# Pooling groups taken in the opposite order, and sums of late modulation vectors folded at wider spacing, in a single-core transformer layer

## The chip, the core and the metric

The kernel runs on one core of a Trainium2 chip. The core has five engines that work side by side: TensorE (PE) multiplies matrices, VectorE (DVE) and ScalarE (ACT) work on whole tiles element by element, GpSimd (POOL) does the same more slowly and issues some of the DMAs, and SyncE (SP) issues the others. Each engine takes its instructions in the order of its own queue. The metric is the time of one execution on the device, in microseconds (us).

## The reference, cut to what matters

The layer updates 256 latent tokens of width 2048, with 256 context tokens beside them. All arithmetic is float32.

```python
mod = silu(c) @ w_mod + b_mod                    # six vectors of 2048: sa, ca, ga, sm, cm, gm
h   = rmsnorm(x) * (1 + ca) + sa                 # the context tokens get their own sa, ca
p   = h @ w_in                                   # q, k, v, pooling input u, gate logits
heads = rmsnorm(diff_attention(q, k, v))         # 8 heads, two softmaxes each
# pooling: u is split in four groups of 256 channels, windows w = 2, 4, 8, 16
for g, w in enumerate((2, 4, 8, 16)):
    lo, hi = clip(t - w // 2, 0, L), clip(t + w - w // 2, 0, L)
    d[g] = window_sum(u[g], lo, hi) / (hi - lo) - u[g]
    y[g] = (d[g] @ pool_w[g]) * pool_scale[g]
mix = (sigmoid(gate_a) * (heads @ w_a_up) + sigmoid(gate_b) * (y @ w_b_up)) @ w_o
x = x + ga * mix
x = x + gm * relu((rmsnorm(x) * (1 + cm) + sm) @ w_ff1) ** 2 @ w_ff2
```

Near either end of the sequence a window is cut off, so that the sum is divided by fewer tokens than w.

## The kernel before, in words

**Products and weight chunks.** Nearly all the time goes into products with weights that are read once. A weight comes as chunks of 128 x 1024 float32 numbers (512 KB). The list `stream`, written by `plan` (L128 to L173), fixes the order of all chunks. For each chunk SP loads a tile `raw` (L117), ACT rounds it to a high part `whi` (L245), and DVE subtracts to get the low part `wlo` (L246). A product is then three products on PE: high by high, high by low and low by high (`mm3`, L276 to L278, and `xstat`, L454 to L460). `wchunk` hands out the next chunk; two chunks ahead of it are loaded and split by then.

**The stages.** Modulation (sa, ca) with the first q and k columns; v, q, k; then, from about 310 us in the trace, `pooling` (16 chunks of w_p), `gates` (four rounds of w_gb_in, w_b, w_ga_in, w_a), the output projection w_o, and the MLP in eight blocks (`ff1`, `ff2`). Attention runs beside the bulk products from v to the first gates: after a fixed amount of bulk work `run` (L870) takes one more step of `attention`. Every second head its clamped squares (`osq`, L727, on POOL) go through a product with a matrix of means (`osum`, L731) for the head norm.

**Pooling.** For a group, four chunks of w_p give u in one PSUM bank (`pin`). ACT copies it into two padded tiles `za` (L786), and POOL adds shifted copies (L791): one add per tile for a window of 2, two for 4, three for 8, four for 16. Some chunks later `pool_diff` does the edge operation on DVE: it multiplies the first w/2 columns (L802) and the last w/2 - 1 columns (L804) by w over the true count, and takes sum / w - u (L806). A window of 2 has no last columns, so its group has no L804. One chunk on, the difference is split into high and low (`split`, L272 and L273), and `pool_out` multiplies it by pool_w. `pool_out` of a group is called two groups later, the last two in the first gates.

**Late modulation.** The vectors ga, cm, sm and gm are needed late, so their weights are slipped between the other chunks at set rates (`late_gen`). DVE multiplies each chunk by its part of silu(c) and adds it up in a tile of 128 partitions (L627, L629), in two halves of 1024 columns per vector. The sum over the 128 partitions is made by seven accumulating DMAs on POOL's queue (`late_fold`, L634), each of which adds the lower half of the partitions that are left to the upper: 64, 32, 16, 8, 4, 2, 1. Then the sum is added to the bias row in DRAM (L637) and broadcast back (L640). Each of these needs the one before to have landed, and POOL waits for that before it issues it. The row's bias is loaded by L619.

**What sets the order.** `later(n, fn)` runs fn when n more chunks have been handed out (`tick`), so it sets the place of fn's instructions in the traced program. From the traced program a planner makes each engine's queue, by when it expects an instruction's operands to be ready; a later traced instruction may go ahead of an earlier one. `pin` holds an instruction behind the one traced just before it on its engine. L802, the additions L627 and L629, the transposes of attention and `osum` are pinned; L804, L806, the splits, POOL's adds and the folds are not.

Of the kernel before, what the change touches and what calls it, by code (L numbers as in the profile page):

```python
# [12 lines left out]
F32R = mybir.dt.float32r  # L13
# [4 lines left out]
P = 128  # L18
# [9 lines left out]
WINDOWS = (2, 4, 8, 16)  # L28
# [20 lines left out]
def layer(ctx: ExitStack, tc, a, out):  # L49
# [22 lines left out]
    def bank(name):  # L72
        return psum.tile([P, 512], F32, tag="ps", name=name)

    def work(name, shape=None, dt=F32):
        return pool.tile(shape or [P, 512], dt, tag="w2", name=name, bufs=9)

    def s16(name, shape, dt=F32):
        return pool.tile(shape, dt, tag="s16", name=name, bufs=7)

    def s8(name, shape, dt=F32):
        return pool.tile(shape, dt, tag="s8", name=name, bufs=2)
# [4 lines left out]
    def pairtile(name):  # L87
        return s16(name, [P, 2, 8, T], F32R)
# [4 lines left out]
    credit_rate = [0.0]  # L93
# [3 lines left out]
    def later(n, fn):  # L97

        waiting.append([n, fn])
# [28 lines left out]
    def plan(name, *idx, rate=0.0):  # L128
        stream.append(((name,) + idx, rate))
# [15 lines left out]
    for n, g, rate in (("w_v", 0, 0.75), ("w_q", 1, 1.0), ("w_k", 1, 1.0), ("w_v", 1, 0.75)):  # L145
        for ch in range(8):
            plan(n, g, ch, rate=0.0 if (n, g) == ("w_v", 1) and ch < 3 else rate)
    for g in range(4):
        for i in range(4):
            plan("w_p", 2 * g + i // 2, i % 2, rate=0.6)  # L150
            if g > 1 and i == 1:
                plan("pool_w", g - 2)
    for g in range(4):
        for n, nk in (("w_gb_in", 8), ("w_b", 4), ("w_ga_in", 8), ("w_a", 4)):
            for ch in range(nk):
                plan(n, g, ch, rate=0.66)
                if g == 0 and n == "w_gb_in" and ch in (1, 7):
                    plan("pool_w", 2 if ch == 1 else 3)
    for g in range(4):
        for ch in range(8):  # L160
            plan("w_o", g, ch, rate=0.6 if g < 2 else 0.0)
# [138 lines left out]
    def pr(name):  # L300
        lo, hi = PRM[name]
        return prm[:, lo:hi]
# [251 lines left out]
    for f in range(KT):  # L554
        if f % 2 == 0:
            ps = bank("mod")
# [40 lines left out]
    def late_gen():  # L597
        for name in ("ga", "cm", "sm", "gm"):
            if name == "ga":
                dst = ga_bc  # L600
            elif name == "gm":
                mods["gm"] = None
                yield
                mods["gm"] = s8("gm_bc", [P, D])
                dst = mods["gm"]
            else:
                if "sb" not in mods:
                    mods["sb"] = s16("sb", [P, 2, D])
                dst = mods["sb"][:, 0 if name == "cm" else 1, :]
            for half in range(2):  # L610
                yield
                o = dst[:, half * 1024:half * 1024 + 1024]
                norm_w = pr("nmw")[:, 8 * half:8 * half + 8] if name == "cm" else None
                for k in range(KT):
                    raw = raw_chunk(a["w_" + name][half, k])
                    later(2 if credit_rate[0] < 1 else 1, partial(late_part, o, raw, k))
                    if k == 8:
                        row = rows.tile([1, 1024], F32, tag="row", name="row")
                        nc.gpsimd.dma_start(row, a["b_" + name][half])  # L619
                    if k == KT - 1:  # L620
                        later(2 if credit_rate[0] < 1 else 1, partial(late_fold, o, row, norm_w, P // 2))
                    yield

    def late_part(o, raw, k):
# [3 lines left out]
        else:  # L628
            pin(vec.scalar_tensor_tensor(o, raw, sil[:, 0, k:k + 1], o, ALU.mult, ALU.add))  # L629

    def late_fold(o, row, norm_w, n):

        if n > 0:
            nc.gpsimd.dma_start(o[0:n, :], o[n:2 * n, :], accum_op=ALU.add)  # L634
            later(2, partial(late_fold, o, row, norm_w, n // 2))
            return
        nc.gpsimd.dma_start(row, o[0:1, :], accum_op=ALU.add)  # L637
        if norm_w is not None:
            later(1, partial(late_norm, row, norm_w))
        later(2 if norm_w is None else 3, lambda: nc.gpsimd.dma_start(o, row.broadcast_to([P, 1024])))  # L640
# [117 lines left out]


    ybh = [None]  # L760
    diff = []

    def pooling():
        yb = pairtile("yb")
        ybh[0] = yb
        diff.clear()
        for g, w in enumerate(WINDOWS):
            ps = bank("pin")
            for i in range(2):
                for kc in range(2):  # L770
                    hi, lo = wchunk("w_p", 2 * g + i, kc)
                    for kk in range(8):
                        k = 8 * kc + kk
                        sl = slice(kk * P, kk * P + P)
                        mm3(ps[:, i * T:i * T + T], hi[:, sl], lo[:, sl], act_slice(hL, k, 0), act_slice(hL, k, 1),
                            k == 0, k == KT - 1)
                    if g > 1 and i == 0 and kc == 1:
                        pool_out(g - 2)
                    yield 2
            s0 = 8 - w // 2  # L780
            sums = []
            for i in range(2):
                src = work("za", [P, T + 16])
                gp.memset(src[:, 0:8], 0.0)
                gp.memset(src[:, T + 8:T + 16], 0.0)
                act.copy(src[:, 8:T + 8], ps[:, i * T:i * T + T])  # L786
                step, n = 1, T + 16
                while step < w:
                    n -= step

                    gp.tensor_add(src[:, 0:n], src[:, 0:n], src[:, step:step + n])  # L791
                    step *= 2
                sums.append(src[:, s0:s0 + T])
            later(3 if g < 3 else 6, partial(pool_diff, g, w, ps, sums))

    def pool_diff(g, w, ps, sums):

        d = work("d")
        n0, n1 = w // 2, w // 2 - 1
        e0 = PRM["edge"][0] + sum(x - 1 for x in WINDOWS[:g]) * 2  # L800
        for i, s in enumerate(sums):
            pin(vec.tensor_mul(s[:, 0:n0], s[:, 0:n0], prm[:, e0:e0 + n0]))  # L802
            if n1:
                vec.tensor_mul(s[:, T - n1:T], s[:, T - n1:T], prm[:, e0 + n0:e0 + n0 + n1])  # L804
            sl = slice(i * T, i * T + T)
            vec.scalar_tensor_tensor(d[:, sl], s, 1.0 / w, ps[:, sl], ALU.mult, ALU.subtract)  # L806
        diff.append((work("dh", dt=F32R), work("dl", dt=F32R)))
        later(1, partial(split, *diff[-1], d))

    def pool_out(g):  # L810
        dh, dl = diff[g]
        wh, wl = wchunk("pool_w", g)
        pd = bank("pd")
        for i in range(2):
            for k in range(2):
                sl = slice(k * T + i * P, k * T + i * P + P)
                mm3(pd[:, i * T:i * T + T], wh[:, sl], wl[:, sl], dh[:, k * T:k * T + T],
                    dl[:, k * T:k * T + T], k == 0, k == 1)
        y = work("py", [P, 2, T])
        for i in range(2):  # L820
            act.activation(y[:, i, :], pd[:, i * T:i * T + T], AF.Copy, scale=pr("pscale")[:, 2 * g + i:2 * g + i + 1])
        split(ybh[0][:, 0, 2 * g:2 * g + 2, :], ybh[0][:, 1, 2 * g:2 * g + 2, :], y)
# [4 lines left out]
    def gates():  # L827

        for g in range(4):
            if g % 2 == 0:  # L830
                mix.append(pairtile(f"mix{g // 2}"))
            part = []
            for gname, wname in (("w_gb_in", "w_b"), ("w_ga_in", "w_a")):
                pg = [bank(f"pg{t}") for t in range(2)]
                for ch, w in enumerate(xstat((gname, g), pg, tokens(2))):
                    if g == 0 and gname == "w_gb_in" and ch == 1:
                        pool_out(2)
                    yield w
                sgm = [work("sgm") for _ in range(2)]
                for t in range(2):  # L840
                    act.activation(sgm[t], pg[t], AF.Sigmoid)
                if g == 0 and gname == "w_gb_in":
                    pool_out(3)
                if wname == "w_a":
                    assert heads[0] == NH
                src = [oT] if wname == "w_a" else [ybh[0]]
                py = [bank(f"pyy{t}") for t in range(2)]
                yield from xstat((wname, g), py, [(src, 0), (src, 1)], nk=4)
                for t in range(2):
                    vec.tensor_mul(sgm[t], sgm[t], py[t])  # L850
                part.append(sgm)
            for t in range(2):
                vec.tensor_add(part[0][t], part[0][t], part[1][t])
            later(4, partial(mix_turn, g, part[0]))
# [330 lines left out]
```

## Time and profile before

| | us |
|---|---|
| median of 3 runs | 1463.2 (1461.52 to 1465.58) |
| the profiled execution, its own time | 1464.75 |
| its span, from the first to the last instruction | 1463.0 |
| PE busy | 1434.3 |
| DVE busy | 983.6 |
| ACT busy | 671.1 |
| POOL busy | 172.5 |

The mean granted clock of PE over the execution is 0.997 of full speed.

A line of a timeline reads: start, duration, engine, line of the kernel, operation, result <- operands, shape, count; in square brackets how long the engine had been idle before it, and what ended that. A line that stands for several instructions gives their whole stretch. A line of waits reads: who waited for whom, total us, times, longest. A line of a stretch of time reads: from:to, length, then busy time (and instructions) of PE, of PE's weight loads, of DVE, ACT and POOL, then the granted clock of PE, the busy share of the DMA engines and GB/s. PE's records overlap, since its matmuls are pipelined. An instruction that issues a DMA from POOL's queue has the POOL line of the kernel and the operation DMA_DIRECT2D; its duration is that of the issue, not of the transfer.

### The profile page before, as it was taken

The numbers are of one execution on the slowest core, as the hardware profiler recorded it, in microseconds if no ns is written. First come the engines' busy times: TensorE is split into PE (matmuls) and PEld (weight loads), VectorE is DVE, ScalarE is ACT, GpSimd is POOL, SyncE is SP. The second block draws the span as 40 slices with busy tenths as digits, with TensorE's granted clock in tenths as the row PEclk, the third lists the DMA queues.
The fourth block names the chain that finished last, engine by engine and source line by source line (L and its number), as shares of the span: only waits on it lengthen the run. The fifth ranks groups of instructions, "written<-read, shape, count | busy, mean of one in ns | idle before, by whom it ended". The sixth has DMA issues, their size and how long they took to land.

```text
span 1463.0 us, 19764 instructions
## 1 busy us (share of the span) xinstructions
PE 1434.3 (98%) x7448; PEld 1179.8 (81%) x7448; DVE 983.6 (67%) x1218; ACT 671.1 (46%) x901; POOL 172.5 (12%) x192
## 2 busy tenths in 40 slices
PE   6999999999799999999999999999999999999998
PEld 4667887788688888888878888888888888888887
DVE  4567785668687777777676656656667465555675
ACT  5235345466454444444445545445344353544432
POOL 1001111111400111010101000010000100000260
PEclk9999999999999999999999999999999999999999
DMA  9996683345699999999756777777777766556563
GB/s 375 409 407 248 214 294 126 112 125 172 180 323 325 334 321 324 329 346 310 217 167 207 235 244 233 237 246 245 248 235 236 208 210 193 189 193 194 184 195 125
DMA packets 100976, 355.23 MB, mean 243 GB/s; under 512 B 12864, under 2 KB 13520, under 8 KB 100880
## 3 DMA queue, kind: packets, MB, share of 16 engines
q1 hardware_dynamic: 96624, 345.19, 69.0%
q0 software_dynamic: 4256, 8.77, 2.8%
q8 instruction: 58, 0.95, 0.3%
q14 instruction: 38, 0.31, 0.1%
HBM read 347.61 MB, written 2.17 MB: 239 GB/s over the span
## 4 chain that ended last, share of the span: by engine, by line
PE 69%; DMA 2%; issue 1%; ACT 0%; POOL 0%; DVE 0%; DVEq 0%; ACTq 0%; POOLq 0%
PE f L1034 13%; PE f L454 8%; PE f L455 8%; PE f L460 8%; PE f L1037 7%; PE pg L460 4%; PE pg L454 4%; PE pg L455 4%; PE pyy L454 2%; PE pyy L455 2%; PE pyy L460 2%; DMA gm_bc<-gm_bc 2%; PE wo L454 1%; PE wo L460 1%; PE wo L455 1%; PE f L276 1%
## 5 line engine op out<-in xcount | busy, mean ns | idle before, releaser
L246 DVE TENSOR_TENSOR wlo<-raw,whi 128x1024 fp32r<-128x1024 f32 (+1 forms) x430 | 536.0, 1249 | 337.1 <-ACT whi L245 308.5
L245 ACT CAST whi<-raw 128x1024 fp32r<-128x1024 f32 (+1 forms) x430 | 449.9, 1048 | 554.2 <-PE f L455 184.5
L1034 PE MATMUL f<-h,whi 128*128 128x512 f32 x896 | 224.4, 392 | 1.0 <-ACT whi L245 1.0
L455 PE MATMUL f<-whi,act 128*128 128x512 f32 x512 | 199.3, 389 | 0.0
L454 PE MATMUL f<-whi,act 128*128 128x512 f32 x512 | 199.2, 389 | 0.0
L1034 PEld LDWEIGHTS f<-h,whi 128*128 128x128 f32 x896 | 161.5, 189 | 30.3 <-ACT whi L245 1.2
L460 PE MATMUL f<-wlo,act 128*128 128x512 f32 x512 | 136.8, 389 | 0.0
L1037 PEld LDWEIGHTS f<-h,wlo 128*128 128x128 f32 x896 | 122.2, 190 | 8.7
L1037 PE MATMUL f<-h,wlo 128*128 128x256 f32 x896 | 124.9, 282 | 0.0
L460 PEld LDWEIGHTS f<-wlo,act 128*128 128x128 f32 x512 | 96.1, 188 | 19.9
L455 PEld LDWEIGHTS f<-whi,act 128*128 128x128 f32 x512 | 96.2, 188 | 19.8
L454 PEld LDWEIGHTS f<-whi,act 128*128 128x128 f32 x512 | 96.2, 188 | 19.7
L454 PE MATMUL pg<-whi,hL 128*128 128x512 f32 x256 | 101.2, 395 | 0.0
L455 PE MATMUL pg<-whi,hL 128*128 128x512 f32 x256 | 99.9, 390 | 0.0
L1045 POOL TENSOR_TENSOR rsq<-relu 128x512 f32<-128x512 f32 x28 | 29.2, 1041 | 433.5 <-ACT relu L1044 423.3
L629 DVE SCALAR_TENSOR_TENSOR sb<-raw,sil,sb 128x1024 f32<-128x1024 f32 x60 | 76.7, 1278 | 0.1
L460 PE MATMUL pg<-wlo,hL 128*128 128x512 f32 x256 | 69.4, 393 | 4.6 <-DVE wlo L246 4.6
L460 PEld LDWEIGHTS pg<-wlo,hL 128*128 128x128 f32 x256 | 48.5, 190 | 15.1 <-DVE wlo L246 5.0
L454 PEld LDWEIGHTS pg<-whi,hL 128*128 128x128 f32 x256 | 48.4, 189 | 10.3 <-issue 0.2
L455 PEld LDWEIGHTS pg<-whi,hL 128*128 128x128 f32 x256 | 48.3, 189 | 10.2 <-issue 0.2
L634 POOL DMA_DIRECT2D sb<-sb x28 | 22.2, 793 | 216.8 <-DMA sb<-sb 114.5
L1059 DVE TENSOR_TENSOR acc<-f,acc 128x512 f32<-128x512 f32 x48 | 30.9, 686 | 20.4 <-PE f L460 20.4
(283 smaller groups left out, 2175.2 us busy)
## 6 DMA issues: line engine op xcount, KB each, us to landing
raw<-in_w_ff_dram SPq DMA_DIRECT2D x240, 512.0 KB, 4.3
raw<-in_w_m_dram SPq DMA_DIRECT2D x64, 512.0 KB, 10.2
raw<-in_w_ga_dram SPq DMA_DIRECT2D x32, 512.0 KB, 4.2
raw<-in_w_gb_in_dram SPq DMA_DIRECT2D x32, 512.0 KB, 5.5
raw<-in_w_cm_dram SPq DMA_DIRECT2D x32, 512.0 KB, 5.3
raw<-in_w_ga_in_dram SPq DMA_DIRECT2D x32, 512.0 KB, 5.2
raw<-in_w_sm_dram SPq DMA_DIRECT2D x32, 512.0 KB, 5.3
raw<-in_w_o_dram SPq DMA_DIRECT2D x32, 512.0 KB, 5.2
```

The costliest lines, as they stand in the source:

```text
L245: act.copy(hi, raw)
L246: vec.tensor_sub(lo, raw, hi.bitcast(F32))
L276: pe.matmul(o, l_hi, r_hi, start=start, stop=False)
L454: pe.matmul(banks[t], tok(h, k, 0, tt), wt, start=k == 0, stop=False)
L455: pe.matmul(banks[t], tok(h, k, 1, tt), wt, start=False, stop=False)
L460: pe.matmul(banks[t], tok(h, k, 0, tt), wt, start=False, stop=k == 2 * nk - 1)
L629: pin(vec.scalar_tensor_tensor(o, raw, sil[:, 0, k:k + 1], o, ALU.mult, ALU.add))
L634: nc.gpsimd.dma_start(o[0:n, :], o[n:2 * n, :], accum_op=ALU.add)
L1034: pe.matmul(ps, hi[:, kk * P:kk * P + P], both(h2, k), start=k == 0, stop=False)
L1037: pe.matmul(ps[:, T:2 * T], lo[:, kk * P:kk * P + P], act_slice(h2, k, 0), start=False, stop=k == KT - 1)
L1045: gp.tensor_mul(sq, r, r)
L1059: vec.tensor_add(acc[:, t, gs], bs[t], acc[:, t, gs])
```

## The change

The four pooling groups are taken in the order 3, 2, 1, 0, so windows of 16, 8, 4 and 2, in `stream` and in `pooling`; `pool_out` of groups 3 and 2 follows in pooling, that of 1 and 0 in the first gates. `pool_diff` of the first three groups taken is due four chunks after the sums instead of three; the last stays at six. `diff` becomes a dictionary, since the groups no longer come in rising order. The steps of `late_fold` are due three chunks apart instead of two for ga, cm and gm, and stay two apart for sm; the first fold, the row and the broadcast keep their own delays.

```diff
-    for g in range(4):
+    for g in reversed(range(4)):
         for i in range(4):
             plan("w_p", 2 * g + i // 2, i % 2, rate=0.6)
-            if g > 1 and i == 1:
-                plan("pool_w", g - 2)
+            if g < 2 and i == 1:
+                plan("pool_w", g + 2)
...
                 if g == 0 and n == "w_gb_in" and ch in (1, 7):
-                    plan("pool_w", 2 if ch == 1 else 3)
+                    plan("pool_w", 1 if ch == 1 else 0)
...
-                        later(2 if credit_rate[0] < 1 else 1, partial(late_fold, o, row, norm_w, P // 2))
+                        later(2 if credit_rate[0] < 1 else 1, partial(late_fold, o, row, norm_w, P // 2, 2 if name == "sm" else 3))
...
-    def late_fold(o, row, norm_w, n):
+    def late_fold(o, row, norm_w, n, step):
 
         if n > 0:
             nc.gpsimd.dma_start(o[0:n, :], o[n:2 * n, :], accum_op=ALU.add)
-            later(2, partial(late_fold, o, row, norm_w, n // 2))
+            later(step, partial(late_fold, o, row, norm_w, n // 2, step))
             return
...
-    diff = []
+    diff = {}
...
-        for g, w in enumerate(WINDOWS):
+        for g, w in reversed(list(enumerate(WINDOWS))):
...
-                    if g > 1 and i == 0 and kc == 1:
-                        pool_out(g - 2)
+                    if g < 2 and i == 0 and kc == 1:
+                        pool_out(g + 2)
...
-            later(3 if g < 3 else 6, partial(pool_diff, g, w, ps, sums))
+            later(4 if g > 0 else 6, partial(pool_diff, g, w, ps, sums))
...
-        diff.append((work("dh", dt=F32R), work("dl", dt=F32R)))
-        later(1, partial(split, *diff[-1], d))
+        diff[g] = work("dh", dt=F32R), work("dl", dt=F32R)
+        later(1, partial(split, *diff[g], d))
...
                     if g == 0 and gname == "w_gb_in" and ch == 1:
-                        pool_out(2)
+                        pool_out(1)
...
                 if g == 0 and gname == "w_gb_in":
-                    pool_out(3)
+                    pool_out(0)
```

## The prediction

> **What bounds the kernel now.** I read first the page's busy times, then the waits of TensorE (PE), then the engines' timelines around its gaps, with stretches of time for the clock.
>
> ```profile
> PE 1434.3 (98%) x7448; PEld 1179.8 (81%) x7448; DVE 983.6 (67%) x1218; ACT 671.1 (46%) x901; POOL 172.5 (12%) x192
> ```
>
> PE is busy for all but 28.7 us of the span. The start and the tail, which the change does not touch, have most of it. The edited stages have three gaps, 8.2 us: the two in brackets here, in pooling and in the first gates, and one of 1.0 us in the MLP (further down). On PE's timeline:
>
> ```profile
> 373.71 0.39 PE L278 MATMUL pin<-hL,wlo 128*128 128x256 f32 x1 [2.66 <-DVE wlo L246]
> ...
> 396.67 2.07 PE L460 MATMUL pg<-wlo,hL 128*128 128x512 f32 x4 [4.56 <-DVE wlo L246]
> ...
> 401.02 1.08 PE L460 MATMUL pg<-wlo,hL 128*128 128x512 f32 x4
> ...
> 403.75 1.07 PE L460 MATMUL pg<-wlo,hL 128*128 128x512 f32 x4
> ...
> 407.38 1.02 PE L731 MATMUL osum<-osq,mean 128*128 128x512 f32 x2
> ```
>
> One gate chunk takes 403.75 - 401.02 = 2.73 us; the one after the long gap took 401.02 - 396.67 = 4.35. The stretches say why, in the granted clock (third number from the end); the first two rows are needed further down:
>
> ```profile
> 332.00:340.00 8.00, 8.00 (x55) 6.50 (x54) 5.87 (x11) 5.62 (x9) 0.00 (x0) 1.00 0.52 175
> 340.00:352.00 12.00, 12.00 (x94) 11.03 (x93) 11.93 (x18) 5.98 (x13) 4.27 (x8) 1.00 0.40 134
> ```
> ```profile
> 372.00:374.00 2.00, 0.29 (x2) 0.30 (x3) 1.99 (x4) 1.45 (x3) 1.10 (x2) 1.00 0.50 128
> 396.00:398.00 2.00, 1.33 (x3) 1.14 (x4) 2.00 (x3) 1.04 (x1) 0.42 (x1) 0.62 0.24 41
> 398.00:400.00 2.00, 2.00 (x6) 1.52 (x6) 2.00 (x3) 0.00 (x0) 0.35 (x1) 0.52 0.80 260
> ```
>
> The 4.56 us gap cost another 4.35 - 2.73 = 1.62 us of slow clock; the 2.66 us gap left it at 1.00. Who made the weight's low part (wlo) late is on VectorE (DVE):
>
> ```profile
> 368.38 1.65 DVE L629 SCALAR_TENSOR_TENSOR ga_bc<-raw,sil,ga_bc 128x1024 f32<-128x1024 f32 x1
> 371.74 0.75 DVE L804 TENSOR_TENSOR za<-za,prm 128x3 f32<-128x3 f32 x2 [1.71 <-POOL za L791]
> 372.43 2.36 DVE L246 TENSOR_TENSOR wlo<-raw,whi 128x1024 fp32r<-128x1024 f32 x2
> ...
> 393.32 0.57 DVE L804 TENSOR_TENSOR za<-za,prm 128x7 f32<-128x7 f32 x1 [9.80 <-POOL za L791]
> ...
> 395.40 2.35 DVE L246 TENSOR_TENSOR wlo<-raw,whi 128x1024 fp32r<-128x1024 f32 x2
> ```
>
> Both times the right-edge multiply L804, which is not pinned, stands in DVE's queue ahead of a weight split (L246) and waits for the window sum on GpSimd (POOL): 1.71 us for the 8-wide group, 9.80 us for the 16-wide one, the last. POOL's timeline shows what that sum waited for:
>
> ```profile
> 367.03 5.26 POOL L791 TENSOR_TENSOR za<-za 128x271 f32<-128x271 f32 x6 [0.36 <-ACT za L786]
> 372.23 0.87 POOL L634 DMA_DIRECT2D ga_bc<-ga_bc  x1
> ...
> 384.05 0.77 POOL L634 DMA_DIRECT2D ga_bc<-ga_bc  x1 [7.01 <-DMA ga_bc<-ga_bc]
> ...
> 388.66 0.80 POOL L634 DMA_DIRECT2D ga_bc<-ga_bc  x1 [3.62 <-DMA ga_bc<-ga_bc]
> 389.21 5.47 POOL L791 TENSOR_TENSOR za<-za 128x271 f32<-128x271 f32 x8
> 394.62 0.78 POOL L634 DMA_DIRECT2D ga_bc<-ga_bc  x1
> ...
> 402.70 1.78 POOL L727 TENSOR_SCALAR osq<-osq 128x512 f32<-128x512 f32 x1
> ```
>
> The folds of the second ga half (L634) each wait for the one before, and POOL's queue with them. The eight adds of the last group come behind the fourth fold, although ACT's copies, their input, were done by 381.1:
>
> ```profile
> 380.68 0.39 ACT L786 COPY za<-pin 128x256 f32<-128x256 f32 x1
> ...
> 391.32 0.60 ACT L726 ACTIVATE osq<-ob 128x512 f32<-128x512 f32 x1
> ```
>
> **The change, part by part.** Instruction counts stay: 20 adds, 6 right-edge and 8 left-edge multiplies, the same folds, and the four pool_w loads in the same places of SP's queue with other contents (no cost). What moves:
>
> *Last place: two adds, no L804.* A 2-wide window has no right edge (n1 = 0), so nothing unpinned on DVE waits for POOL there. Its pinned L802 comes four gate chunks into the next stage, where the adds have long ended even behind the folds. The 4.56 us gap and its 1.62 us of slow clock go: **-6.18** (if another instruction takes L804's place in the queue, 0).
>
> *Third place: four adds instead of six.* 5.26 x 4/6 = 3.5 us, so done at 370.5 instead of 372.3. DVE is free at 368.38 + 1.65 = 370.03, so L804 ends near 370.7 and the first split, 2.36 / 2 = 1.18 long, near 371.9 instead of 373.6. The gap shrinks by **1.7** (bounds 0 and 2.66).
>
> *First place: eight adds instead of two, now with an L804.* The two adds there ran beside a full DVE:
>
> ```profile
> 327.68 2.91 POOL L791 TENSOR_TENSOR za<-za 128x271 f32<-128x271 f32 x2 [1.63 <-ACT za L786]
> ```
> ```profile
> 332.00 0.68 DVE L693 TENSOR_REDUCE mx<-sc 128x1 f32<-128x512 f32 x1
> ```
>
> That is 1.46 us each, against 5.47 / 8 = 0.68 beside an idle one. If L804 is put into DVE's first hole, at 332.00 + 0.68 = 332.7, then 5.0 / 1.46 = 3.4 adds are done, and the others need 4.6 x 0.68 = 3.1 us while DVE waits. DVE idles 8.00 - 5.87 = 2.1 us before 340 anyway; the other 1.0 us would be pushed into 340 to 352, where it is busy 11.93 of 12. At 1.46 for all eight the wait is 6.7 us and 4.6 pass. Taken: **+0.5**, between 0 (weights split early enough) and 1.0; the bound of 4.6 stays for the range.
>
> [...]
>
> *Pooling's edge work one chunk later, groups 3, 2 and 1.* L802 is pinned behind the last DVE instruction traced before it, so it, the division, the split of d and the bank of the group's sums all go back by one chunk. In first place dl was done early:
>
> ```profile
> 345.72 0.67 DVE L273 TENSOR_TENSOR dl<-d,dh 128x512 fp32r<-128x512 f32 x1
> ```
> ```profile
> 350.89 0.28 PE L276 MATMUL pd<-dh,whi 128*128 128x256 f32 x1
> ```
>
> 4.5 us of cover against one chunk. Taken 0, up to +1.0 if the cover ends.
>
> *Folds due three chunks apart (ga, cm, gm).* A due time sets where a fold is traced, not when it is issued. Counted from the listing, the first ga half's broadcast (L640) is due 16 chunks after its first fold, the rope adds (L485) of w_k already 8 after it; yet:
>
> ```profile
> 233.17 0.57 POOL L640 DMA_DIRECT2D ga_bc<-row  x1 [2.56 <-DMA row<-ga_bc]
> 256.54 1.29 POOL L485 TENSOR_TENSOR qraw<-qraw,qsq 128x512 f32<-128x512 f32 x1 [22.80 <-DVE rq_t L288]
> ```
> ```profile
> L619 POOL DMA_DIRECT2D row<-in_b_gm_dram x2: 486/486/486, 8.4 to 9.6; - x2
> ```
>
> The gm bias rows, due hundreds of chunks in, went out at 8 to 10 us. POOL's order follows readiness, so the spacing alone is worth **0**. In the gm stage the last folds kept ACT from a split for 7.18 us (next row) and PE, by its waits, for 1.0 us (second row); bounds -1.0 (gone) and +1.0 (a second square held).
>
> ```profile
> 1170.60 0.62 ACT L272 CAST act<-rsq 128x512 fp32r<-128x512 f32 x1 [7.18 <-POOL rsq L1045]
> ```
> ```profile
> PE f L1034 <- ACT whi L245: 1.0, 1, 1.0
> ```
>
> *What is late next.* PE reaches osum (407.38 before) 6.18 + 1.7 - 0.5 = 7.4 us earlier, at 400.0. Its operand is the clamp L727 (fed by ACT's L726), which stood behind the folds and ended at 402.70 + 1.78. The chain starts 1.7 earlier (372.23 less 1.7), so its fourth fold is at 387.0; the fifth follows 388.66 - 384.05 = 4.6 later at 391.6 (two adds fit between), 3.0 earlier than 394.62. The clamp then ends at 401.5: PE waits 1.5. But folds are not always so quick; in the later gates the three after a fourth took 492.20 - 477.81 = 14.4 us:
>
> ```profile
> 477.81 0.80 POOL L634 DMA_DIRECT2D sb<-sb  x1 [3.69 <-DMA sb<-sb]
> ...
> 492.20 0.79 POOL L634 DMA_DIRECT2D sb<-sb  x1 [3.35 <-DMA sb<-sb]
> ```
>
> From 387.0 that is 401.4, and with 0.8 of issue and 1.8 of clamp 404.0: a wait of 4.0. If the clamp overtakes a fold, 0. Taken: **+2.0**, near the shorter case.
>
> Sum: -6.18 - 1.7 + 0.5 + 2.0 = **-5.4 us**. Against the profiled execution's 1464.75 that is 1459.4; that execution lay 1.55 above the median of 1463.2, so the median becomes 1457.8, about **1458**.
>
> **The rivals.**
>
> *A. No wait at osum.* The clamp goes ahead of the last folds: -7.4, 1455.8. For it: the clamp's input is ready at 391.32 + 0.60 (quoted above), before the fifth fold. Against: in the run before all seven folds stood ahead of it, three of them issued after its input was ready.
>
> *B. The wait moves.* osum waits the full 4.0 and the clock falls again (1.62), and the first group passes 1.0: -6.18 - 1.7 + 1.0 + 5.6 = -1.3, 1462. For it: the fold times of the later gates. Against: at 2.66 us of idling the clock stayed.
> [...]
>
> *C. Slower: due times do bind.* If POOL issues folds at their chunk, the first ga half's last fold and its row step, due 18 and 21 chunks after its first instead of 12 and 14, fall around the first group's eight adds, due after 20. Two fold waits of 4.6 ahead of sums that DVE waits for: 9.2 + 3.1 - 2.1 = 10.2 us reach PE, with 1.62 of clock and 2.0 at osum: -7.88 + 13.8 = +5.9, 1469. It passes zero from 3.3 us of fold wait on. Against it: the rows at 233.17 and 8.4.
>
> **How the numbers follow.** Forecast 0.42, A 0.27, B 0.19, C 0.12. A measurement of this kernel tells 0.3% (4.4 us, 1458.8 and 1467.6) from no change. The forecast lies 1.0 below that line: two thirds of it (0.28) and A (0.27) are faster, 0.55. Its other third (0.14), B (0.19) and the mild end of C (0.02) are no change, 0.35; the rest of C is slower, 0.10. Lowest: no osum wait, third gap and gm wait gone, -6.18 - 2.66 - 1.0 = -9.8, 1453.4. The range goes from 1453.5 to 1466, past B, and leaves out most of C; the forecast's own is 1456 to 1460.
>
> **What would show it.** No gap behind DVE L246 and a clock of 1.00 near 390; L804's waits short and in the first group only; the gap at w_p's last group near 1 us; a PE wait for POOL osq at L731 of 0 (A), about 2, or 4 (B); POOL's broadcast of the first ga half again before the w_k rope adds (not C). The prediction is wrong if an L804 of any group waits over 5 us, or if the gates show a new PE wait over 3 us.

## The result, and the profile after

The changed kernel takes 1469.86 us (median of 8 runs, 1467.0 to 1472.94) against 1463.61 for the kernel before (8 runs, 1461.52 to 1465.58): a ratio of 1.0043, 95% interval 1.0031 to 1.0055. It is slower by 6.3 us. The forecast of 1458 and its range are wrong, and so is the sign. The ratios compare fast executions; two far slower ones of the kernel before (1591 and 2912 us, run beside four of the experiments) are left out.

The profiled execution of the changed kernel took 1468.2 us, with a span of 1466.4. It is 3.45 us above the profiled one of before, while the two medians are 6.3 apart: the profiled execution of before lay 1.1 us above its kernel's median of 8, that of the changed kernel 1.7 below its own. What moves single executions by so much is not shown here.

The waits of PE in the changed kernel (us in total, times, longest):

```profile
PE ssq L68 <- DVE sq L68: 10.7, 3, 7.0
PE pyy L454 <- ACT yb L272: 3.9, 1, 3.9
PE pd L277 <- DVE dl L273: 2.5, 1, 2.5
...
PE osum L731 <- POOL osq L727: 2.0, 1, 2.0
...
PE pd L276 <- ACT dh L272: 0.5, 1, 0.5
PE pyy L455 <- DVE yb L273: 0.3, 1, 0.3
```

The waits for wlo in pooling and in the first gates are gone, and so is the one for whi in the MLP. Three new ones stand in their place. On PE's timeline:

```profile
350.77 0.28 PE L278 MATMUL pin<-hL,wlo 128*128 128x256 f32 x1
351.57 0.39 PE L276 MATMUL pd<-dh,whi 128*128 128x256 f32 x1 [0.52 <-ACT dh L272]
354.45 0.58 PE L277 MATMUL pd<-dl,whi 128*128 128x256 f32 x1 [2.50 <-DVE dl L273]
...
360.11 0.28 PE L276 MATMUL pin<-hL,whi 128*128 128x256 f32 x1
360.23 0.28 PE L277 MATMUL pin<-hL,whi 128*128 128x256 f32 x1
...
405.68 1.13 PE L731 MATMUL osum<-osq,mean 128*128 128x512 f32 x2 [2.05 <-POOL osq L727]
...
417.61 0.85 PE L454 MATMUL pyy<-whi,yb 128*128 128x512 f32 x2 [3.92 <-ACT yb L272]
418.77 1.22 PE L455 MATMUL pyy<-whi,yb 128*128 128x512 f32 x2 [0.32 <-DVE yb L273]
...
422.40 0.39 PE L454 MATMUL pyy<-whi,yb 128*128 128x512 f32 x1
```

The granted clock (third number from the end) in two stretches:

```profile
352.00:354.00 2.00, 0.00 (x0) 0.00 (x0) 2.00 (x3) 0.46 (x1) 2.00 (x3) 0.80 0.47 123
...
358.00:360.00 2.00, 2.00 (x12) 2.00 (x11) 1.05 (x3) 1.51 (x3) 0.00 (x0) 0.50 0.58 217
...
418.00:420.00 2.00, 1.68 (x5) 1.04 (x4) 1.85 (x3) 0.00 (x0) 0.00 (x0) 0.51 0.82 268
```

Behind pd's wait the clock stays at half until 360.0. From 354.45 to 360.11 PE starts 26 matmuls in 5.66 us; at the 0.12 us of the rows from 360.11 on they take 3.1, so 2.5 us are lost. The first w_b chunk takes 422.40 - 417.61 = 4.79 us, with the small wait of 0.32 in it, which is 2.06 more than the 2.73 of a gate chunk before. With the waits of before that are gone, the books of the two profiled executions are:

| | us |
|---|---|
| third group's wait for wlo, and a small one ahead of it | -2.66 - 0.28 |
| last group's wait for wlo, its slow clock | -4.56 - 1.62 |
| MLP's wait for whi | -1.0 |
| pd, two waits, slow clock | +0.52 + 2.50 + 2.5 |
| osum | +2.05 |
| first w_b product, wait, its slow first chunk | +3.92 + 2.06 |
| sum (measured 3.45) | +3.4 |

DVE shows why pd waited:

```profile
333.70 0.85 DVE L804 TENSOR_TENSOR za<-za,prm 128x7 f32<-128x7 f32 x2 [3.59 <-POOL za L791]
...
339.87 1.22 DVE L246 TENSOR_TENSOR wlo<-raw,whi 128x1024 fp32r<-128x1024 f32 x1 [0.18 <-ACT whi L245]
...
353.28 1.12 DVE L273 TENSOR_TENSOR dl<-d,dh 128x512 fp32r<-128x512 f32 x1
```

L804 of the 16-wide group, now in first place, holds DVE for 3.59 us. The split that starts here at 339.87 started at 335.68 before, so DVE is 4.2 us late, and dl, the low part of the first group's difference, at 345.72 before, comes at 353.28.

ACT shows what the first w_b product waited for:

```profile
412.48 1.28 ACT L841 ACT_TABLE_LOAD   x1
...
415.26 0.84 ACT L821 ACTIVATE py<-pd,prm 128x256 f32<-128x256 f32 x2
...
416.91 0.65 ACT L272 CAST yb<-py 128x512 fp32r<-128x512 f32 x1
```

The last row is the high part of the last pool_out. PE had finished that product at 413.41 + 0.28 = 413.69, but ACT took its result (L821) only at 415.26, behind the sigmoids of the gates with the load of their table (L841), and rounded it (L272) behind one more weight. On PE this pool_out stands directly ahead of the first w_b product, whose first chunk multiplies channels 0 to 255, those of group 0. In the natural order the last pool_out is that of group 3, which w_b reads in its last chunk; in the new order it is that of group 0.

POOL, from the first group to osum's clamp:

```profile
327.68 6.66 POOL L791 TENSOR_TENSOR za<-za 128x271 f32<-128x271 f32 x8 [1.64 <-ACT za L786]
...
371.00 3.73 POOL L791 TENSOR_TENSOR za<-za 128x271 f32<-128x271 f32 x4 [0.71 <-ACT za L786]
374.68 0.87 POOL L634 DMA_DIRECT2D ga_bc<-ga_bc  x1
...
399.11 0.77 POOL L634 DMA_DIRECT2D ga_bc<-ga_bc  x1 [2.37 <-DMA ga_bc<-ga_bc]
...
400.12 1.23 POOL L791 TENSOR_TENSOR za<-za 128x271 f32<-128x271 f32 x2
403.26 0.81 POOL L634 DMA_DIRECT2D ga_bc<-ga_bc  x1 [1.90 <-DMA ga_bc<-ga_bc]
403.87 1.76 POOL L727 TENSOR_SCALAR osq<-osq 128x512 f32<-128x512 f32 x1
```

The last group's two adds stand behind six folds (four before), and the clamp behind all seven. The clamp ends at 405.63, against 404.48 before.

### The profile page after: what moved, and what is told of

It reads as the page before. It is cut to its first block, busy times and chain, and to the rows that moved or that the text cites. A ratio compares the mean times of both kernels' runs of the same rounds, so it can differ in the third digit from the quotient of the medians.

```text
span 1466.4 us, 19766 instructions
## 1 busy us (share of the span) xinstructions
PE 1437.5 (98%) x7448; PEld 1182.9 (81%) x7448; DVE 987.3 (67%) x1218; ACT 671.2 (46%) x901; POOL 170.9 (12%) x192
## 4 chain that ended last, share of the span: by engine, by line
PE 69%; DMA 1%; DVE 0%; ACT 0%; issue 0%; DVEq 0%; ACTq 0%
PE f L1034 14%; PE f L454 8%; PE f L455 8%; PE f L460 8%; PE f L1037 7%; PE pg L454 3%; PE pg L455 3%; PE pg L460 3%; PE pyy L455 2%; PE pyy L460 2%; PE pyy L454 2%; PE wo L455 1%; PE wo L454 1%; PE wo L460 1%; PE f L276 1%; PE f L277 1%
```

## The experiments

Ratios are to the kernel before, run beside each experiment on the same chip, with 95% intervals; its medians there were 1464.1 to 1465.2 us. An edit that adds lines shifts the line numbers behind it, so that in some rows the clamp is L731 and osum L735; the names of the tiles tell them apart.

**The spacing of the folds.** Once taken out of the change, once alone.

```diff
-                        later(2 if credit_rate[0] < 1 else 1, partial(late_fold, o, row, norm_w, P // 2, 2 if name == "sm" else 3))
+                        later(2 if credit_rate[0] < 1 else 1, partial(late_fold, o, row, norm_w, P // 2, 2))
```

This is the edit to the changed kernel. The other way, the lines of `late_fold` and its call in the change were put into the kernel before by themselves.

> The changed kernel with the folds of all modulation sums two chunks apart again. Theory 1 (GpSimd issues folds as they become ready, the due time has no part in it): the same order of folds and adds, the time within 1.5 us of 1469.9. Theory 2 (the wider spacing is what put six folds ahead of the last group's adds and so made the osum wait of 2.05 us, or what took the 1.0 us gap out of the MLP's modulation stage): osum's wait gone, 2 us less; or a wait of 1.0 us for whi there again, 1 us more.

> The kernel before with the folds three chunks apart, and nothing else of the change. Theory 1 (due times do not bind): 1463.6 within 1.0 us, the long gap ahead of the last group and the 1.0 us gap in the MLP's modulation stage as before. Theory 2 (the spacing alone takes the MLP gap away): 1462.6. Theory 3 (due times bind and the folds get in the way of the sums): over 1465.

Measured 1.0046 (1.0033 to 1.006) without it and 1.0004 (0.9992 to 1.0016) alone. In the first the adds of the last group stand behind six folds and osum waits 1.9, as in the changed kernel. The wait for whi in the MLP is back at 1.0 there, which is what theory 2 said; but with the wide spacing alone it stays at 1.0 too, and in all other experiments it was 0.7 to 2.1 us, with either spacing. So its absence from the changed kernel's profile is no gain of the change, and the spacing has no measurable effect.

**The last group's channels read last.** The first w_b product reads its chunks backwards.

```diff
-            for ch in range(nk):
+            for ch in (reversed(range(nk)) if (n, g) == ("w_b", 0) else range(nk)):
                 plan(n, g, ch, rate=0.66)
...
-        for ch in range(nk - last + 1):
-            n = last if ch == nk - last else 1
+        back = w == ("w_b", 0)
+        for at in range(nk - last + 1):
+            ch = nk - 1 - at if back else at
...
```

The lines left out move the marks of the product's first and last matmul to the chunks that are now first and last. The product has four chunks; inside a chunk the order stays, so that it is not quite the "15 down to 0" of the expectation.

> The changed kernel, but the first w_b product reads its chunks backwards (k from 15 down to 0), so that the channels of the group whose pool_out comes last are read last. Theory 1 (the reversal put the last pool_out in front of the very first w_b matmul, which reads that group's channels): the wait of TensorE at pyy (3.92 + 0.32 us) and the slow clock behind it (about 2.0) go: 6.2 us less than the changed kernel's 1469.9, 1463.7, and no pyy wait over 0.5. Theory 2 (the time only moves on, to the end of that product or to the next one): pyy's wait appears at a later matmul and the time stays within 1.5 us of 1469.9.

Measured 0.9993 (0.9984 to 1.0002): 0.0050, or 7.3 us, under the changed kernel. The wait at pyy is gone and no other wait in the gates took its place. Theory 1 holds, at a price somewhat over its 6.2.

**The edge work at three chunks again.**

```diff
-            later(4 if g > 0 else 6, partial(pool_diff, g, w, ps, sums))
+            later(3 if g > 0 else 6, partial(pool_diff, g, w, ps, sums))
```

> The changed kernel, but the edge work of groups 3, 2 and 1 is due three chunks later again instead of four. Theory 1 (the wait for the first group's difference, 3.0 us of TensorE at pd with about 2.3 us of slow clock behind it, comes from two delays added up, 4.2 us that VectorE idled for the sums and about 3.3 us of the extra chunk, against 5.2 us of cover): dl ends about 3.3 us earlier, near 351, pd waits at most 0.5 and the time is 5.3 us less than 1469.9: 1464.6. Theory 2 (the 4.2 us of lateness alone use up the cover, because weight splits and folds stand ahead of the edge work wherever it is traced): pd still waits over 2 us and the time stays within 1.5 us of 1469.9.

Measured 1.0053 (1.004 to 1.0066); theory 1 falls in its time. Its mechanism was half right. Two rows of DVE and one of PE:

```profile
350.20 0.67 DVE L273 TENSOR_TENSOR dl<-d,dh 128x512 fp32r<-128x512 f32 x1
...
354.01 1.12 DVE L246 TENSOR_TENSOR wlo<-raw,whi 128x512 fp32r<-128x512 f32 x1
```
```profile
355.18 0.58 PE L278 MATMUL pd<-dh,wlo 128*128 128x256 f32 x1 [3.61 <-DVE wlo L246]
```

dl came in time, but the split of pool_w, which stands behind it on DVE, was late in its turn and PE waited 3.61 us for that. DVE as a whole was late, by its 3.59 at L804, which this kernel has too. The last group's adds stood behind four folds again, but osum still waited 3.54 us.

**The edge work one chunk later, alone**, in the kernel before.

```diff
-            later(3 if g < 3 else 6, partial(pool_diff, g, w, ps, sums))
+            later(4 if g < 3 else 6, partial(pool_diff, g, w, ps, sums))
```

> The kernel before with the edge work of its first three groups due four chunks later instead of three, and nothing else of the change. Theory 1 (the 4.5 us between the first group's difference and its use cover one chunk): no new wait at pd, within 1.0 us of the kernel before. Theory 2 (a chunk costs more than the cover, because folds and a weight split come ahead of the difference): a wait at pd of 1 to 3 us and 1.001 to 1.003 of the time before.

Measured 1.0024 (1.0013 to 1.0035), with no wait at pd: each theory is half right. The price is elsewhere. POOL, DVE, PE:

```profile
395.33 0.77 POOL L634 DMA_DIRECT2D ga_bc<-ga_bc  x1 [3.77 <-DMA ga_bc<-ga_bc]
396.34 4.64 POOL L791 TENSOR_TENSOR za<-za 128x271 f32<-128x271 f32 x7
```
```profile
399.72 0.58 DVE L804 TENSOR_TENSOR za<-za,prm 128x7 f32<-128x7 f32 x1 [9.42 <-POOL za L791]
402.53 0.58 DVE L804 TENSOR_TENSOR za<-za,prm 128x7 f32<-128x7 f32 x1 [2.23 <-POOL za L791]
```
```profile
404.90 2.08 PE L460 MATMUL pg<-wlo,hL 128*128 128x512 f32 x4 [5.28 <-DVE wlo L246]
```

The last group's adds went back from behind the fourth fold to behind the sixth (the last add even behind the seventh), as in the changed kernel. Their input came later: ACT's last copy for the group ended at 386.98, against 381.07 before. Whether this alone makes the planner place them there was not tried.

**L804 pinned**, in the changed kernel, in the kernel before, and in the changed kernel with w_b backwards.

```diff
-                vec.tensor_mul(s[:, T - n1:T], s[:, T - n1:T], prm[:, e0 + n0:e0 + n0 + n1])
+                pin(vec.tensor_mul(s[:, T - n1:T], s[:, T - n1:T], prm[:, e0 + n0:e0 + n0 + n1]))
```

> The changed kernel with the right-edge multiply L804 pinned behind the left-edge multiply L802, so that VectorE cannot reach it before the edge work is due. Theory 1 (the pd wait comes from the 4.2 us that VectorE lost at L804 waiting for the first group's eight adds; the run with the edge work at three chunks kept a wait of that size and only changed the operand that was late): no L804 wait, VectorE's first weight split after it back near 336, no pd wait over 0.5, 5.3 us (0.36%) less than the changed kernel: 1.0007 of the time before. Theory 2 (the wait comes from the edge work's place, behind folds and splits, and not from L804): pd still waits 2 to 4 us, 1.004.

> The kernel before with L804 pinned behind L802 and nothing else changed. Theory 1 (the two gaps in pooling and the first gates were VectorE held by the unpinned L804, and the order of the groups has no part in them): the gaps of 2.66 and 4.56 us and 1.6 us of slow clock go, osum then waits 2 to 4 us for the clamp behind the folds: 5 to 7 us less, 0.995 to 0.9965 of the time before. Theory 2 (the wait only moves, to osum in full with a slow clock, or to the last group's pd, whose sums stand behind the folds on GpSimd): within 2 us, 0.9985 to 1.0015.

> The changed kernel with L804 pinned and the first w_b product reading its chunks backwards. Theory 1 (the loss is the sum of two separate mechanisms, VectorE's wait at L804 in first place and the last group's channels read first): 5.3 and 7.3 us less than the changed kernel, 1.0043 - 0.0036 - 0.0050 = 0.9957, and TensorE's only wait over 1 us in pooling and the first gates is osum's, near 2. Theory 2 (VectorE's lateness and the product's wait overlap, or a third operand is late once both are gone): 0.999 to 1.000.

Measured 1.0059 (1.0042 to 1.0077), 1.0039 (1.0024 to 1.0054) and 1.0015 (1.0002 to 1.0028). The local part of every first theory is right: pd does not wait in the first and third, and the 4.56 us gap is gone in the second. Yet the pin gained nothing: the third is 0.0022 above the same kernel without it, and the second 0.0039 above the kernel before. PE in the three, in that order:

```profile
406.42 2.08 PE L731 MATMUL osum<-osq,mean 128*128 128x512 f32 x2 [7.72 <-POOL osq L727]
```
```profile
410.50 2.08 PE L731 MATMUL osum<-osq,mean 128*128 128x512 f32 x2 [10.96 <-POOL osq L727]
```
```profile
407.06 2.07 PE L735 MATMUL osum<-osq,mean 128*128 128x512 f32 x2 [7.55 <-POOL osq L731]
```

Whatever PE saves ahead of osum, it spends there, and the clock falls besides: from 404 to 408 it is 0.50 in all three. In the kernel before, osum started at 407.38 without a wait. In all ten kernels so far it is between 404 and 411, and in all of them the clamp comes behind seven folds, each waiting for the transfer of the one before it. First and last fold, and clamp, of the second:

```profile
374.62 0.88 POOL L634 DMA_DIRECT2D ga_bc<-ga_bc  x1
...
408.08 0.80 POOL L634 DMA_DIRECT2D ga_bc<-ga_bc  x1 [4.18 <-DMA ga_bc<-ga_bc]
408.66 1.78 POOL L727 TENSOR_SCALAR osq<-osq 128x512 f32<-128x512 f32 x1
```

From the first fold to the last there are 29.9 us before (372.23 to 402.12), 28.6 in the changed kernel and 33.5 here. The new theory: this chain bounds the stretch, and the gap of 4.56 us was one of the places where its wait could stand.

**osum ten chunks behind the clamp**, in the third of these kernels.

```diff
-            later(5, norm)
+            later(10 if h == NH - 1 else 5, norm)
```

> The changed kernel with L804 pinned, the first w_b product backwards, and the sum over squares of the last head pair (osum) ten chunks behind its clamp instead of five. Theory 1 (what came free in the run without the last edit was eaten by osum, which stood 7.55 us at the clamp that GpSimd holds behind the folds, with about 2.5 us of slow clock): that wait goes and nothing takes its place: 1.0015 - 0.0068 = 0.9947 of the time before. Theory 2 (the folds hold the last group's adds too, so its pool_out is the next to wait): 2 to 4 us at pd, 0.9965 to 0.998. Theory 3 (osum's wait is a sign of something else that is late, the modulation sums' loads for instance): 1.0 to 1.002 with a wait of the same size at the next product.

Measured 0.9995 (0.9983 to 1.0007), between theories 2 and 3. The chain found a third way to PE:

```profile
402.76 0.58 DVE L806 TENSOR_TENSOR za<-za,prm 128x1 f32<-128x1 f32 x1 [8.21 <-POOL za L795]
```
```profile
407.12 2.07 PE L464 MATMUL pg<-wlo,hL 128*128 128x512 f32 x4 [4.04 <-DVE wlo L246]
```

The left-edge multiply (L802, here L806) of the last group waits 8.21 us for adds behind the folds, with the weight splits queued behind it. This kernel also has a wait of 1.95 us for a whi at 438.71, which none of the others has; its cause was not followed.

**The folds behind the clamp.** The first fold of the second ga half is traced after the last clamp and pinned behind it; the other six follow it anyway.

```diff
-                    if k == KT - 1:
+                    if k == KT - 1 and name == "ga" and half == 1:
+                        behind_clamp.append(partial(late_fold, o, row, norm_w, P // 2, hold=pin))
+                    elif k == KT - 1:
...
-            nc.gpsimd.dma_start(o[0:n, :], o[n:2 * n, :], accum_op=ALU.add)
+            hold(nc.gpsimd.dma_start(o[0:n, :], o[n:2 * n, :], accum_op=ALU.add))
...
+            if h == NH - 1:
+                behind_clamp.pop()()
```

It was put into the kernel before, alone and with L804 pinned, and into the changed kernel with L804 pinned and w_b backwards.

> The kernel before with one edit: the first fold of the second ga half is traced after the last head pair's clamp and pinned behind it, so that GpSimd has the last group's adds and the clamp ahead of all folds of that half. Theory 1 (the fold chain on GpSimd is what bounds the stretch from the last pooling group to osum, through the adds or through the clamp): L804 of the last group waits under 3 us, osum does not wait, the 4.56 us gap and its slow clock are gone, 6.2 us less: 0.9958 of the time before; the 2.66 us gap of the third group stays, since no fold stands ahead of its adds. Theory 2 (the folds are only moved to where the next sums, those of cm, wait for them, or the lower queue makes VectorE's next work late): within 2 us, 0.9985 to 1.0015.

> The kernel before with the folds of the second ga half behind the last clamp, and L804 pinned behind L802. Theory 1 (pinning lost in the run without the folds moved only because osum then stood 11.0 us at the clamp): all three gaps of pooling and the first gates are gone, 6.2 + 2.9 us less: 0.994 of the time before, 0.01 under the run with the pin alone. Theory 2 (the pin itself costs, by keeping VectorE from the edges in its holes): over 0.998.

> The changed kernel with L804 pinned, the first w_b product backwards, and the folds of the second ga half behind the last clamp. Theory 1 (three mechanisms make up the changed kernel's loss: VectorE held in first place 5.3 us, the last group's channels read first 6.2 to 7.3, osum behind the folds): no wait of TensorE over 1 us in pooling and the first gates, 0.994 of the time before, level with the natural order with the same folds (so the order of the groups is worth nothing once the folds are out of the way). Theory 2 (eight adds beside a full VectorE in first place cost time that the natural order does not pay): 0.996 to 0.999.

Measured 0.9968 (0.9955 to 0.9982), 0.9951 (0.9931 to 0.997) and 0.9941 (0.9924 to 0.9958). POOL, and PE's third group, in the first:

```profile
380.78 7.16 POOL L797 TENSOR_TENSOR za<-za 128x271 f32<-128x271 f32 x8 [2.72 <-ACT za L792]
392.37 4.07 POOL L731 TENSOR_SCALAR osq<-osq 128x512 f32<-128x512 f32 x1 [4.43 <-ACT osq L730]
396.39 0.88 POOL L638 DMA_DIRECT2D ga_bc<-ga_bc  x1
...
429.76 0.79 POOL L638 DMA_DIRECT2D ga_bc<-ga_bc  x1 [3.94 <-DMA ga_bc<-ga_bc]
```
```profile
374.05 0.38 PE L278 MATMUL pin<-hL,wlo 128*128 128x256 f32 x1 [2.67 <-DVE wlo L246]
```

Adds and clamp run as soon as ACT delivers, osum has no wait, and of the gaps over 1 us in pooling and the first gates only that of 2.67 is left, as expected. With the pin it shrinks to 0.66, and osum has no wait there either. In the third kernel no wait in pooling and the first gates is over 1 us. It is the fastest of all, 1455.86 us on a chip where the kernel before took 1464.17; its interval and the second's overlap, so these runs show no value of either order.

**The parts of the change with the folds out of the way.** Three kernels with the last edit: the changed kernel with w_b backwards, the changed kernel alone, and the kernel before with the edge work one chunk later.

> The changed kernel with the folds of the second ga half behind the last clamp and the first w_b product backwards; L804 stays unpinned. Theory 1 (VectorE's 3.59 us at L804 in first place is a loss of its own, hidden so far because osum had to wait for the clamp anyway): pd waits about 3 us with a slow clock behind it, 5.3 us more than the same kernel with the pin (0.9941): 0.9977 of the time before. Theory 2 (the lateness is taken up somewhere by VectorE's idle time): 0.994.

> The changed kernel with the folds of the second ga half behind the last clamp, and nothing else. Theory 1 (the three mechanisms add up): pd's 5.3 us and the 6.2 us at the first w_b product stay, osum's 2.05 go: 0.9941 + 0.0036 + 0.0042 = 1.002 of the time before. Theory 2 (the folds held everything, and the two other waits shrink with them): under 0.998.

> The kernel before with the edge work of its first three groups due four chunks later instead of three, and the folds of the second ga half behind the last clamp. Theory 1 (the extra chunk cost 0.24% only because the last group's buffers came free later, so that its adds fell behind six folds instead of four): level with the same kernel at three chunks, 0.9968 within 0.001. Theory 2 (the extra chunk has a price without the folds as well): 0.9968 + 0.0024 = 0.9992.

Measured 0.9979 (0.9968 to 0.9991), 1.0021 (1.0012 to 1.003) and 0.9963 (0.9948 to 0.9979): theory 1 each time, the first two within 0.0002 of its figure. The waits of PE in the second:

```profile
PE pyy L454 <- ACT yb L272: 3.9, 1, 3.9
PE pd L277 <- DVE dl L273: 2.5, 1, 2.5
```

So DVE's waits at L804 cost 0.0038 (0.9979 less 0.9941; 3.59 us in first place, and 1.13 in third place, which the pin removes too), and the last group's channels 0.0042 (1.0021 less 0.9979), where nothing downstream absorbs them. The extra chunk, in the natural order, has no measurable cost once the folds stand elsewhere.

## Why the prediction was wrong, point by point

In the profile two terms turn the sign: the wait at the first w_b product with its slow chunk, 5.98 us, which the sum did not have, and pd's 5.52, where it had 0.5. Behind them stands a third error: the gains ahead of osum were counted against a clamp that did not come as early as forecast.

- **Last place, -6.18.** Right that no L804 waits there and that the gap goes; wrong that this is worth its length. It was the folds' wait, standing at L804, and osum was next in line for it. In the kernel before, osum came 407.38 - 404.48 = 2.90 us after the clamp's end; with the clamp 1.15 later, only 1.7 could be gained up to osum, and it did start 1.70 earlier (405.68). The remark that L802 comes when the adds have long ended was wrong too: they ended at 401.35, and it waited 1.16 us.
- **Third place, -1.7.** The wait is gone whole (2.66), in a kernel in which PE was already late; with the pin, where PE does not wait at pd, 0.38 of it remains.
- **First place, +0.5.** A mis-sized term. The wait at L804 was 3.59, forecast 3.1. The step that failed let the 2.1 us that DVE idled before 340 take up most of the delay: those holes are waits for ACT that come back behind the delay (0.84, 0.85 and the 0.18 at 339.87, against 0.85, 0.85 and 0.18 before), so DVE was 4.2 us late and not 1.0. Pinning it away is worth 0.0038, 5.6 us, where the folds allow it; the bound of 4.6 left out the slow clock. That bound rested on 1.46 us an add beside a working DVE; the eight adds with the pin took 0.96 each.
- **Edge work, 0.** Taken alone its local claim holds: no wait at pd. Two steps failed. The 4.5 us of cover were held against one chunk only, not against first place's lateness in the same queue: dl came 4.2 + 3.4 = 7.6 us later. And the cost on POOL, two more folds ahead of the last group's adds, was not worked out at all; alone it makes 0.24%.
- **Spacing, 0.** Right, by two runs.
- **osum, +2.0.** The measured 2.05 is right by accident. The clamp ended at 405.63, against 401.5 to 404.0 in the forecast, and PE arrived at 403.63 instead of 400.0, held up by pd. With pd's wait pinned away osum waits 7.72. The step that failed is the start of the chain: "1.7 earlier" than 372.23 became 374.68, because the four adds ahead of it started at 371.00, and even with pd mended 372.79. In that last kernel the four adds started at 367.14, as the six did before, but took 5.70 us instead of the 3.5 forecast, with DVE at work beside them.
- **Not in the sum: the order in which w_b reads the groups.** The part that counted "the four pool_w loads in the same places" stopped there, and did not ask who reads the result of the last one. That missing term is 3.92 + 2.06 in the profile and 0.0042 to 0.0050 in the ratios, alone enough to use up the forecast's -5.4. It is also the sign that the prediction had named for being wrong, a new wait of PE over 3 us in the gates.
- **Rivals.** A did not come: the clamp stayed behind all seven folds. C gave the right time, 1469, by a mechanism that is not there: the first ga half's broadcast came at 233.23, 0.06 us from where it was, and the spacing does nothing. B named what the runs with the pin show, a wait that moves to osum with a slow clock. Its price of 4.0 was too low for that case.
- **The clock.** The forecast counted no slow clock for its wait of 2.0 us at osum, B did for its 4.0. By the length of the gap the runs agree: gaps of 2.05, 2.66 and 2.67 us left the clock at 1.00, those of 3.61 and 3.92 us took it to 0.50. The time of idling before the fall was not the same each time. Ahead of 354.45, in pd's wait of 2.50, the clock fell at 353.2, 2.15 us after 350.77 + 0.28 and with a matmul of pd in between; in the gap of 3.61 us it fell 2.1 us after PE had stopped, and in that of 4.56 us before the change 4.4 us after.

## What to carry to other kernels

A gap ends with whatever is late last. Before counting its length as a gain, follow what the late operand itself stood behind: if that is a chain in another engine's queue, ask what else stands behind it and where PE meets that next; here the chain's end set osum's time, and beyond the 2.9 us by which the clamp had been early, every gap ahead of it was only a place to wait. When independent items are put in a new order, look up who reads the last one first. And hold an operand's cover against the sum of all delays in its engine's queue, not against each edit by itself.

## What the runs showed of the hardware that was not expected

- Once down, the clock stayed down for 3.4 us (396.5 to 399.9 in the kernel before, 418.0 to 421.4 in the changed one), 6.8 (353.2 to 360.0 behind pd's wait) or 13.7 (401.9 to 415.6 in the kernel before with L804 pinned). So the same stall had more than one price. The two waits at pd, 3.0 us, cost another 2.5 of slow clock in the changed kernel's profile; in that of the changed kernel with the folds behind the clamp the clock was down from 354.0 to 357.4 only: 22 matmuls took 4.25 us (353.11 to 357.36) instead of 2.6, so that 1.6 were lost.
- The folds' time did not fall with what is transferred: the steps run from 64 partitions down to 1, and the waits between them in the changed kernel are 3.37, 7.30, 3.12, 4.28, 2.37 and 1.90 us; from the first issue to the last the seven of the second ga half took 27.8 to 33.5 us in all 17 kernels, ahead of the clamp or behind it (396.39 to 429.76 in the kernel before with only that edit).
- The same adds took longer in some places than in others: the first group's eight took 6.66 us in the changed kernel, where DVE stood waiting for them for 3.59, and 7.64 there with L804 pinned and DVE at work; the last group's eight took 5.47 in the kernel before and 10.33 in the kernel before with the folds behind the clamp and L804 pinned.
